# Block 1's small matmuls: heads and index scores in alternating row groups and banks, compression sums in column groups, attention in pairs of units

## The chip, the cores and the metric

The kernel runs on one core of one Trainium2 chip. The metric is the device time of one execution in microseconds; a time is the median of several runs. The profile is of one further execution, whose own time stands beside its span.

## The reference

Two transformer blocks on 256 tokens of width 1024, in float32. The change lies in the first block's mixer. Cut to what it touches:

```python
# DSA: index scores choose the 64 keys that each query of 8 heads attends to
s_h = einsum('bqhd,bsd->bqhs', qi, k_i)              # 8 index heads of width 32
score = einsum('bqh,bqhs->bqs', wi, relu(s_h))       # causal
_, idx = top_k(score, 64)
logits = einsum('bqhd,bqkd->bqhk', qa, k_a[idx]) / 8 + bias   # heads of width 64, one shared key
o_a = softmax(logits) @ v_a[idx]
# NSA: 8 heads of width 64 in two groups, each with its own keys; three branches, gated
k_cmp = gelu(blocks(kc) @ w1_k) @ w2_k               # 15 blocks of 32 tokens, stride 16; same for v
o_c = softmax(q @ k_cmp / 8 + bias) @ v_cmp
o_s = softmax(q @ k_s / 8 + bias) @ v_s              # all 4 blocks are selected at 256 tokens
o_w = softmax(q @ k_w / 8 + bias) @ v_w
mix = sigmoid(gate_a) * (o_a @ w_branch_a) + sigmoid(gate_b) * ((g0*o_c + g1*o_s + g2*o_w) @ w_branch_b)
```

## The kernel before, in words

Weights stream from HBM in units of two k-tiles (`stream_dma`, on SP's queue) into four raw buffers; ScalarE and VectorE split each into a rounded part `hi` (L262) and a remainder `lo` (L263). `gemm_feat` (L337) runs a chunk of 512 columns as 8 k-tiles, each of 4 feature tiles by 3 matmuls (`hi`·`xh`, `hi`·`xl`, `lo`·`xh`; L349, L351, L352) of 256 columns.

Small work is put between the gemms' k-tiles by hand: `later` appends jobs to a list, and a gemm takes one job off it behind each of its first seven k-tiles (`flush(1)`); `flush()` takes all that is left. In block 1 the input gemm's chunks run in the order 4, 0, 1, 3, 2 and then the four gate chunks 5 to 8. Jobs in their order:

- beside chunk 1 and on: eight `index(t, hp)` jobs, each with two matmuls of 32 rows (head group `hp` lies at partitions 32·hp), a relu on ScalarE and two score additions on VectorE; then eight `topk(r)` jobs on VectorE;
- appended behind chunk 1: `bias_job`, a matmul whose result `tv` goes to DRAM and comes back as the bias table `BT` by eight transfers of POOL's queue, followed on POOL by a memset and two copies into `cmpB`, which wait for those transfers;
- beside chunk 2: `cmp1(i, half)`, 16 accumulating matmuls of 30 columns for each of k and v, the gelu, whose output `ge` POOL clears first (L756), then `cmp2`;
- beside the gate chunks: `cq` (compressed logits), then the attention as `step(i)` over 18 units. A unit is two heads of 256 keys or four heads of 128 keys. `step(i)` runs `qk` of unit i (L835, 64 rows), `pv` of unit i-3 (L868) and `tr` of unit i-2 (transposes, L855). VectorE adds the bias and takes the maximum (L841), ScalarE takes the exponent (L846), VectorE copies the transposes (L857).

The order of instructions on TensorE, VectorE and ScalarE is planned from a simulated timeline, so it can deviate from the order of the code; POOL and SP keep the order of the code. PSUM's eight banks are three for gemm sums (`acc`), two for transposes (`tr`), two for small results (`sm`) and one for outputs (`o`). While `wide` is set, every other transpose group takes an `sm` bank (`ptr`).

Of the kernel before, what the change touches and what calls it, by code (L numbers as in the profile page):

```python
# [9 lines left out]
F32 = mybir.dt.float32  # L10
# [199 lines left out]
class Prog:  # L210
# [342 lines left out]
    def block1_mix(self, x0, x):  # L553
        tc, nc, ap, g = self.tc, self.nc, self.ap, self.g
        with ExitStack() as es, ExitStack() as rs_:
# [100 lines left out]
            def index(t, hp):  # L656
                n = 128 * (t + 1)
                pr = slice(32 * hp, 32 * hp + 32)
                ps = self.psm().rearrange("p (a b) -> p a b", a=2)
                for a in range(2):  # L660
                    nc.tensor.matmul(ps[:, a, :n], qi[pr, a, t * 128:t * 128 + 128], ki[pr, :n], start=True,
                                     stop=True)
                R = ip.tile([128, 2, 256], F32, tag="R", name="R")
                nc.scalar.activation(R[:, :, :n], ps[:, :, :n], AF.Relu, scale=1.0 / 16)
                if hp == 2:
                    cur[t] = caus[:, 256 - n:]
                for a in range(2):
                    h = hp + 4 * a
                    nx = ip.tile([128, 256], F32, tag="sc%d" % t, name="sc")
                    nc.vector.scalar_tensor_tensor(nx[:, :n], R[:, a, :n], wi(t, h), cur[t], op0=ALU.mult,  # L670
                                                   op1=ALU.add)
                    cur[t] = nx[:, :n]
# [19 lines left out]
            mp = rpool("cmpp", 1)  # L692
            cw = []
# [8 lines left out]
            def d1(i, ps):  # L702
# [3 lines left out]
                for i, nm in enumerate("kv"):  # L706
# [5 lines left out]
                    blk = mp.tile([128, 16, 2, 15], F32, name="blk" + nm)  # L712
                    for gr in range(2):
                        v = bass.AP(tensor=kp.tensor, offset=kp.offset + 256 * gr,
                                    ap=[list(kp.ap[0]), [2, 16], [16, 15]])
                        nc.gpsimd.tensor_tensor(blk[:, :, gr, :], v,
                                                cw[i][1][:, 0:16].unsqueeze(2).to_broadcast([128, 16, 15]),
                                                op=ALU.add)
# [60 lines left out]
            self.later(lambda: cmp1(0, 0), lambda: cmp1(0, 1), lambda: cmp1(1, 0), lambda: cmp1(1, 1),  # L779
# [25 lines left out]
            units = []  # L805
            for br in (1, 2, 0):
                for t in (1, 0):
                    nh = 2 if t else 4
                    for u in range(8 // nh):
                        if br == 0:  # L810
                            pr, fts = 64 * (u % 2), [nh * (u // 2) + i for i in range(nh)]
                            heads = [2 * f + u % 2 for f in fts]
                        else:
                            heads = [nh * u + i for i in range(nh)]
                            pr, fts = 64 * (heads[0] // 4), [h % 4 for h in heads]
                        units.append(dict(br=br, t=t, nh=nh, pr=pr, fts=fts, heads=heads, first=(u == 0),
                                          last=(u == 8 // nh - 1)))
# [10 lines left out]
            def qk(U):  # L828
                br, t, nh, pr = U["br"], U["t"], U["nh"], U["pr"]
                n, j0 = 128 * (t + 1), 128 - 128 * t  # L830
                q = qa if br == 0 else qb
                kk = ka[pr:pr + 64, :n] if br == 0 else kv[pr:pr + 64, 1 + br, :n]
                ps = self.psm().rearrange("p (a b) -> p a b", a=nh)
                for i in range(nh):
                    nc.tensor.matmul(ps[:, i, :], q[pr:pr + 64, U["fts"][i], t * 128:t * 128 + 128], kk, start=True,  # L835
                                     stop=True)
# [91 lines left out]
            extra = {2: [ct], 4: [lambda: cv(1), lambda: cv(0)]}  # L928
# [3 lines left out]
            nu = len(units)  # L932
            n_nsa = sum(1 for U in units if U["br"])
            for i in range(4):
                extra.setdefault(n_nsa + 4 + i, []).append(jb[i])
# [12 lines left out]
            for i in range(nu + 3):  # L948
                steps.append(lambda i=i: step(i))
# [14 lines left out]
            self.flush()  # L964
            for t in range(2):
# [616 lines left out]
```

## Time and profile before

| | us |
|---|---|
| median of 3 runs (1139.65 to 1142.34) | 1141.07 |
| profiled execution, its own time | 1140.78 |
| span of that execution | 1139.0 |
| TensorE busy in the span | 1112.4 (98%) |
| VectorE busy | 766.9 (67%) |
| ScalarE busy | 573.3 (50%) |
| POOL busy | 143.8 (13%) |

PE is TensorE's matmul row and PEld its weight loads, DVE is VectorE, ACT ScalarE. A busy PE is a pipeline with work in it, so the distance from one matmul's start to the next says more than a matmul's own duration. PEclk is the granted share of the full clock of 2.4 GHz.

### The profile page before, as it was taken

What the parts mean: (1) busy time and instruction counts of PE and PEld (TensorE: products, weight loads), DVE (VectorE), ACT (ScalarE), POOL (GpSimd) and SP (SyncE); (2) the same over time, 40 slices, a digit from 0 to 9 for tenths busy, and PEclk for the clock granted to TensorE, in tenths of its full rate; (3) what the DMA queues carried; (4) which work ended last, traced back from release to release, by engine and by line L of the source; (5) the groups of instructions that cost most, each with busy time, mean ns of one, the idle gap of its engine ahead of it and who ended that gap; (6) DMA issues with size and microseconds to landing.
All of it is one profiled execution on the core that took longest, in us unless ns stands there. A gap on an engine that the chain in (4) does not pass through costs nothing.

```text
span 1139.0 us, 17655 instructions
## 1 busy us (share of the span) xinstructions
PE 1112.4 (98%) x6848; PEld 993.6 (87%) x6848; DVE 766.9 (67%) x1208; ACT 573.3 (50%) x858; POOL 143.8 (13%) x145
## 2 busy tenths in 40 slices
PE   8989999999999999999999999999999999999997
PEld 8888899888888888888878998889999987888886
DVE  6755776778764568777457676556779777776644
ACT  6324454555544446555446335555555455655542
POOL 1411230000000010000001784000323000000000
PEclk9998999999999999999999999999999998999999
DMA  8792214655555655555555655434545455555552
GB/s 294 255 195 97 65 51 146 200 187 187 191 196 173 201 181 187 186 184 192 195 167 184 192 179 167 162 119 145 185 149 166 166 188 167 185 186 186 188 179 92
DMA packets 55876, 196.91 MB, mean 173 GB/s; under 512 B 6700, under 2 KB 6972, under 8 KB 55536
## 3 DMA queue, kind: packets, MB, share of 16 engines
q1 hardware_dynamic: 52704, 186.44, 49.9%
q0 software_dynamic: 2800, 9.21, 3.3%
q8 instruction: 54, 0.88, 0.3%
q14 instruction: 30, 0.25, 0.1%
q10 hardware_dynamic: 288, 0.14, 0.1%
HBM read 192.84 MB, written 1.44 MB: 171 GB/s over the span
## 4 chain that ended last, share of the span: by engine, by line
PE 85%; POOL 5%; DMA 4%; DVE 4%; ACT 1%; issue 1%; DVEq 0%; SPq 0%; POOLq 0%; ACTq 0%
PE acc L368 20%; PE acc L369 10%; PE acc L307 9%; PE acc L306 9%; PE acc L305 9%; PE acc L349 6%; PE acc L351 6%; PE acc L352 6%; PE sm L835 2%; POOL sw L1261 2%; DMA sw<-qkT 2%; POOL qkT L1262 2%; POOL qkT L1260 1%; PE o L868 1%; DVE lo L263 1%; DMA BT<-tvd 1%
## 5 line engine op out<-in xcount | busy, mean ns | idle before, releaser
L263 DVE TENSOR_TENSOR lo<-raw,hi 128x1024 fp32r<-128x1024 f32 (+2 forms) x356 | 450.0, 1267 | 272.1 <-ACT hi L262 270.2
L262 ACT ACTIVATE hi<-raw 128x1024 fp32r<-128x1024 f32 (+2 forms) x356 | 371.5, 1045 | 432.9 <-issue 133.4
L368 PE MATMUL acc<-xs,hi 128*128 128x512 f32 x960 | 340.3, 400 | 1.3 <-DVE sum L374 1.1
L369 PE MATMUL acc<-xs,lo 128*128 128x256 f32 x960 | 269.0, 281 | 1.6 <-DVE lo L263 1.6
L368 PEld LDWEIGHTS acc<-xs,hi 128*128 128x128 f32 x960 | 180.8, 189 | 44.6 <-DVE sum L374 1.3
L349 PE MATMUL acc<-xs,hi 128*128 128x256 f32 (+1 forms) x696 | 199.8, 289 | 0.3 <-ACT hi L262 0.3
L351 PE MATMUL acc<-xs,hi 128*128 128x256 f32 (+1 forms) x696 | 199.0, 287 | 0.0
L352 PE MATMUL acc<-xs,lo 128*128 128x256 f32 (+1 forms) x696 | 198.1, 287 | 0.1
L369 PEld LDWEIGHTS acc<-xs,lo 128*128 128x128 f32 x960 | 181.9, 189 | 2.3 <-DVE lo L263 1.9
L349 PEld LDWEIGHTS acc<-xs,hi 128*128 128x128 f32 (+1 forms) x696 | 133.6, 192 | 3.7 <-issue 2.5
L351 PEld LDWEIGHTS acc<-xs,hi 128*128 128x128 f32 (+1 forms) x696 | 133.7, 192 | 2.4 <-issue 2.0
L352 PEld LDWEIGHTS acc<-xs,lo 128*128 128x128 f32 (+1 forms) x696 | 132.9, 192 | 1.6 <-issue 1.0
L306 PE MATMUL acc<-lo,hT 128*128 128x512 f32 x304 | 118.5, 390 | 0.0
L307 PE MATMUL acc<-hi,hT 128*128 128x512 f32 x304 | 118.0, 389 | 0.0
L305 PE MATMUL acc<-hi,hT 128*128 128x512 f32 x304 | 117.8, 390 | 0.0
L307 PEld LDWEIGHTS acc<-hi,hT 128*128 128x128 f32 x304 | 57.1, 188 | 11.9
L305 PEld LDWEIGHTS acc<-hi,hT 128*128 128x128 f32 x304 | 57.1, 188 | 11.8
L306 PEld LDWEIGHTS acc<-lo,hT 128*128 128x128 f32 x304 | 57.1, 188 | 11.7
L305 PE MATMUL acc<-hi,xs 128*128 128x386 f32 (+1 forms) x128 | 48.6, 381 | 1.6 <-DVE f L1129 1.5
L306 PE MATMUL acc<-lo,xs 128*128 128x386 f32 (+1 forms) x128 | 47.9, 374 | 0.0
L307 PE MATMUL acc<-hi,xs 128*128 128x386 f32 (+1 forms) x128 | 47.0, 373 | 0.0
L374 DVE TENSOR_TENSOR sum<-acc,sum 128x512 f32<-128x512 f32 x60 | 41.1, 684 | 0.0
(421 smaller groups left out, 1396.6 us busy)
## 6 DMA issues: line engine op xcount, KB each, us to landing
raw<-in_w_in SPq DMA_DIRECT2D x100, 512.0 KB, 3.5
raw<-in_ffn_w_gate SPq DMA_DIRECT2D x44, 512.0 KB, 3.4
raw<-in_ffn_w_up SPq DMA_DIRECT2D x44, 512.0 KB, 3.3
raw<-in_ffn_w_down SPq DMA_DIRECT2D x44, 512.0 KB, 3.4
raw<-in_w_mlp_in SPq DMA_DIRECT2D x32, 512.0 KB, 3.4
raw<-in_w_mlp_out SPq DMA_DIRECT2D x32, 512.0 KB, 3.3
raw<-in_w_out SPq DMA_DIRECT2D x16, 512.0 KB, 3.5
raw<-in_w_in SPq DMA_DIRECT2D x16, 386.0 KB, 3.3
```

The costliest lines, as they stand in the source:

```text
L262: nc.scalar.activation(hi[:, :n * w], raw[:, :n * w], AF.Copy)
L263: nc.vector.tensor_tensor(lo[:, :n * w], raw[:, :n * w], hi[:, :n * w], op=ALU.subtract)
L305: nc.tensor.matmul(ps[t][:, :w], xh[:, k, sl], hi, start=(k == 0), stop=False)
L306: nc.tensor.matmul(ps[t][:, :w], xh[:, k, sl], lo, start=False, stop=False)
L307: nc.tensor.matmul(ps[t][:, :w], xl[:, k, sl], hi, start=False, stop=last)
L349: nc.tensor.matmul(o, hi[:, fs], xh[:, k, :], start=(k == 0 and f % 2 == 0), stop=False, skip_group_check=True)
L351: nc.tensor.matmul(o, hi[:, fs], xl[:, k, :], start=False, stop=False, skip_group_check=True)
L352: nc.tensor.matmul(o, lo[:, fs], xh[:, k, :], start=False, stop=last, skip_group_check=True)
L368: nc.tensor.matmul(ps[:, f, :, :], hi[:, fs], x.both[:, k, :, :], start=(k == 0), stop=False)
L369: nc.tensor.matmul(ps[:, f, 0, :], lo[:, fs], x.hi[:, k, :], start=False, stop=last)
L374: nc.vector.tensor_tensor(s, ps[:, :, 0, :], s, op=ALU.add)
L835: nc.tensor.matmul(ps[:, i, :], q[pr:pr + 64, U["fts"][i], t * 128:t * 128 + 128], kk, start=True, stop=True)
```

## The change

Four things are edited. `index` takes two head groups at once, each with a bank of its own, and issues their matmuls in turn, so that neighbours lie in different row groups. `cmp1` swaps stationary and moving operands: the 32 columns of a block (30 and two zeros) are loaded, the 128 columns of `w1` move, and the 16 partial products go to four column groups, l mod 4; `cmp1b` then adds the four groups up by a matmul with `fold`, four stacked identities that POOL copies at the start. The attention pairs units into nine duos whose two halves lie in the two row groups; `qk` issues their matmuls in turn into two banks, `step(i)` runs `pv` of duo i-2, `qk` of duo i and `tr` of duo i-1, each step is followed by one empty place or one transposition job, and `narrow()` keeps transposes off the `sm` banks until the gate chunks are done.

```diff
-            def index(t, hp):
+            def index(t, hps):
                 n = 128 * (t + 1)
-                pr = slice(32 * hp, 32 * hp + 32)
-                ps = self.psm().rearrange("p (a b) -> p a b", a=2)
+                pss = [self.psm().rearrange("p (a b) -> p a b", a=2) for _ in hps]
                 for a in range(2):
-                    nc.tensor.matmul(ps[:, a, :n], qi[pr, a, t * 128:t * 128 + 128], ki[pr, :n], start=True,
-                                     stop=True)
+                    for hp, ps in zip(hps, pss):
+                        pr = slice(32 * hp, 32 * hp + 32)
+                        nc.tensor.matmul(ps[:, a, :n], qi[pr, a, t * 128:t * 128 + 128], ki[pr, :n], start=True,
+                                         stop=True)
...
-                for hp in (2, 0, 1, 3):
-                    self.later(lambda t=t, hp=hp: index(t, hp))
+                for hps in ((2, 0), (1, 3)):
+                    self.later(lambda t=t, hps=hps: index(t, hps))
...
+            fold = mp.tile([128, 32], F32, name="fold")
+            for q in range(4):
+                nc.gpsimd.tensor_copy(fold[32 * q:32 * q + 32, :], self.ident[32 * q:32 * q + 32, 32 * q:32 * q + 32])
...
-                    blk = mp.tile([128, 16, 2, 15], F32, name="blk" + nm)
+                    blk = mp.tile([128, 16, 32], F32, name="blk" + nm)
+                    nc.gpsimd.memset(blk[:, :, 30:32], 0.0)
...
-            def cmp1(i, half):
+            def cmp1(i):
                 nm = "kv"[i]
-                if half == 0:
-                    cps[i] = self.psm()
-                ps = cps[i]
-                for l in range(8 * half, 8 * half + 8):
-                    nc.tensor.matmul(ps[:, :30], cw[i][0][:, l, :], blks[i][:, l, :, :].rearrange("p a b -> p (a b)"),
-                                     start=(l == 0), stop=(l == 15))
-                if half == 0:
-                    return
+                ps = self.psm()
+                for l4 in range(4):
+                    for q in range(4):
+                        l = 4 * l4 + q
+                        nc.tensor.matmul(ps[32 * q:32 * q + 32, :128], blks[i][:, l, :], cw[i][0][:, l, :],
+                                         start=(l4 == 0), stop=(l4 == 3), skip_group_check=True)
+                hq = mp.tile([128, 128], F32, name="hq" + nm)
+                nc.vector.tensor_copy(hq, ps[:, :128])
+                cps[i] = hq
+
+            def cmp1b(i):
+                nm = "kv"[i]
+                ps = self.psm()
+                nc.tensor.matmul(ps[:, :32], cps[i], fold, start=True, stop=True)
...
-            self.later(lambda: cmp1(0, 0), lambda: cmp1(0, 1), lambda: cmp1(1, 0), lambda: cmp1(1, 1),
+            self.later(lambda: cmp1(0), lambda: cmp1(1), None, lambda: cmp1b(0), lambda: cmp1b(1), None,
                        lambda: cmp2(0), lambda: cmp2(1))
...
+            duos = []
             for br in (1, 2, 0):
                 for t in (1, 0):
                     nh = 2 if t else 4
+                    for u in range(4 // nh):
+                        fts = [nh * u + i for i in range(nh)]
+                        duo = []
+                        for half in range(2):
+                            heads = [2 * f + half for f in fts] if br == 0 else [f + 4 * half for f in fts]
+                            duo.append(dict(br=br, t=t, nh=nh, pr=64 * half, fts=fts, heads=heads,
+                                            first=(u == 0 and half == 0), last=(u == 4 // nh - 1 and half == 1)))
+                        duos.append(duo)
...
+            def qk(duo):
+                pss = [self.psm().rearrange("p (a b) -> p a b", a=duo[0]["nh"]) for _ in duo]
+                for i in range(duo[0]["nh"]):
+                    for U, ps in zip(duo, pss):
+                        br, t, pr = U["br"], U["t"], U["pr"]
+                        n = 128 * (t + 1)
+                        q = qa if br == 0 else qb
+                        kk = ka[pr:pr + 64, :n] if br == 0 else kv[pr:pr + 64, 1 + br, :n]
+                        nc.tensor.matmul(ps[:, i, :], q[pr:pr + 64, U["fts"][i], t * 128:t * 128 + 128], kk,
+                                         start=True, stop=True)
+                for U, ps in zip(duo, pss):
+                    softmax(U, ps)
...
-            extra = {2: [ct], 4: [lambda: cv(1), lambda: cv(0)]}
+            extra = {1: [ct], 2: [lambda: cv(1), lambda: cv(0)]}
...
             def step(i):
-                if i + 2 < nu and units[i + 2]["br"] == 0:
-                    bm(units[i + 2])
-                if i < nu:
-                    qk(units[i])
-                if 0 <= i - 3 < nu:
-                    pv(units[i - 3])
-                if 0 <= i - 2 < nu:
-                    tr(units[i - 2])
+                if 0 <= i - 2 < nu:
+                    for U in duos[i - 2]:
+                        pv(U)
+                if i + 1 < nu and duos[i + 1][0]["br"] == 0:
+                    for U in duos[i + 1]:
+                        bm(U)
+                if i < nu:
+                    qk(duos[i])
+                if 0 <= i - 1 < nu:
+                    for U in duos[i - 1]:
+                        tr(U)
                 for e in extra.get(i, ()):
                     e()
-            for i in range(nu + 3):
-                steps.append(lambda i=i: step(i))
+            for i in range(nu + 2):
+                steps += [lambda i=i: step(i), jb[i - n_nsa - 2] if 0 <= i - n_nsa - 2 < 4 else None]
+            steps += jb[len(duos) - n_nsa:]
+            self.narrow()
             self.later(*steps)
...
             self.flush()
+            self.wide = True
```

## Rows read from the trace of the kernel before

**Rows 1.** The page: busy time of TensorE; its granted clock in 40 slices.

```profile
PE 1112.4 (98%) x6848; PEld 993.6 (87%) x6848; DVE 766.9 (67%) x1208; ACT 573.3 (50%) x858; POOL 143.8 (13%) x145
...
PEclk9998999999999999999999999999999998999999
```

**Rows 2.** Stretches: length, busy of PE, PEld, DVE, ACT, POOL, clock, DMA share, GB/s.

```profile
28.00:57.00 29.00, 29.00 (x208) 25.88 (x206) 22.97 (x49) 11.30 (x16) 13.15 (x24) 1.00 0.75 253
57.00:81.40 24.40, 24.40 (x204) 23.55 (x202) 16.14 (x49) 6.36 (x8) 5.40 (x10) 1.00 0.90 189
81.40:87.60 6.20, 0.12 (x2) 0.00 (x0) 0.22 (x3) 0.07 (x1) 0.91 (x5) 0.86 0.71 167
87.60:92.60 5.00, 4.97 (x39) 4.74 (x40) 2.18 (x3) 3.14 (x11) 0.27 (x1) 0.50 0.34 107
...
96.60:176.00 79.40, 79.40 (x585) 71.44 (x585) 56.65 (x175) 37.78 (x118) 18.70 (x16) 1.00 0.21 68
```

**Rows 3.** Waits of TensorE, 20 to 200 us: in all, times, longest.

```profile
PE sm L766 <- DVE gek L757: 6.1, 1, 6.1
```

**Rows 4.** Chain of waits, 58 to 90 us: start, length, what.

```profile
60.38 0.46 DVE tv L591
...
71.16 15.15 DMA BT<-tvd
...
86.69 0.38 POOL cmpB L600
...
87.29 0.07 POOL gek L756
...
87.63 0.40 PE sm L766 x4
88.03 0.56 PE sm L773 x16
```

**Rows 5.** Timeline of PE, 32 to 34 us: start, length, line, operation, count.

```profile
32.09 0.28 PE L351 MATMUL acc<-xs,hi 128*128 128x256 f32 x1
32.21 0.28 PE L352 MATMUL acc<-xs,lo 128*128 128x256 f32 x1
32.42 1.13 PE L661 MATMUL sm<-ki,qi 32*128 32x256 f32 x4
...
33.70 0.28 PE L351 MATMUL acc<-xs,hi 128*128 128x256 f32 x1
```

**Rows 6.** Timeline of PE around an index job of 128 columns.

```profile
42.45 0.28 PE L351 MATMUL acc<-xs,hi 128*128 128x256 f32 x1
42.66 0.71 PE L661 MATMUL sm<-ki,qi 32*128 32x128 f32 x4
...
43.52 0.28 PE L349 MATMUL acc<-xs,hi 128*128 128x256 f32 x1
```

**Rows 7.** Timeline of PE around the heads of one unit.

```profile
121.84 0.28 PE L352 MATMUL acc<-xs,lo 128*128 128x256 f32 x1
122.05 1.13 PE L835 MATMUL sm<-kv,qb 64*128 64x256 f32 x4
...
123.33 0.28 PE L351 MATMUL acc<-xs,hi 128*128 128x256 f32 x1
```

**Rows 8.** All head passes (L835): count, ns min/median/max, first and last start, forms.

```profile
L835 PE MATMUL sm<-kv,qb x64: 272/374/480, 96.6 to 142.3; 64*128 64x256 f32 x32, 64*128 64x128 f32 x32
...
L835 PE MATMUL sm<-ka,qa x32: 272/374/480, 144.9 to 165.1; 64*128 64x256 f32 x16, 64*128 64x128 f32 x16
```

**Rows 9.** The passes of cmp2's second half (L773), same columns.

```profile
L773 PE MATMUL sm<-csv,gev x16: 290/314/314, 88.0 to 88.3; 128*16 128x64 f32 x16
```

**Rows 10.** Timeline of PE around one half of a compression sum.

```profile
66.55 0.28 PE L352 MATMUL acc<-xs,lo 128*128 128x256 f32 x1
66.67 1.86 PE L743 MATMUL sm<-blkk,w1k 128*128 128x30 f32 x16
...
68.57 0.28 PE L351 MATMUL acc<-xs,hi 128*128 128x256 f32 x1
```

More of the change, by code (lines that the diff above doesn't have):

```diff
@@ L654, in block1_mix @@
             cur = {}
-            def index(t, hp):
+            def index(t, hps):
                 n = 128 * (t + 1)
-                pr = slice(32 * hp, 32 * hp + 32)
-                ps = self.psm().rearrange("p (a b) -> p a b", a=2)
+                pss = [self.psm().rearrange("p (a b) -> p a b", a=2) for _ in hps]
                 for a in range(2):
-                    nc.tensor.matmul(ps[:, a, :n], qi[pr, a, t * 128:t * 128 + 128], ki[pr, :n], start=True,
-                                     stop=True)
[L663 to L672, printed above, removed]
+                    for hp, ps in zip(hps, pss):
+                        pr = slice(32 * hp, 32 * hp + 32)
+                        nc.tensor.matmul(ps[:, a, :n], qi[pr, a, t * 128:t * 128 + 128], ki[pr, :n], start=True,
+                                         stop=True)
+                for hp, ps in zip(hps, pss):
+                    R = ip.tile([128, 2, 256], F32, tag="R", name="R")
+                    nc.scalar.activation(R[:, :, :n], ps[:, :, :n], AF.Relu, scale=1.0 / 16)
+                    if hp == 2:
+                        cur[t] = caus[:, 256 - n:]
+                    for a in range(2):
+                        h = hp + 4 * a
+                        nx = ip.tile([128, 256], F32, tag="sc%d" % t, name="sc")
+                        nc.vector.scalar_tensor_tensor(nx[:, :n], R[:, a, :n], wi(t, h), cur[t], op0=ALU.mult,
+                                                       op1=ALU.add)
+                        cur[t] = nx[:, :n]
             def topk(r):
@@ L808, in block1_mix @@
                     nh = 2 if t else 4
[L809 to L817, printed above, removed]
+                    for u in range(4 // nh):
[6 more added lines that the diff above has]
+                        duos.append(duo)
             box = {}
@@ L826, in bm, with softmax @@
                                         M[:, t, :n].unsqueeze(1).to_broadcast([128, nh, n]), op=ALU.add)
-            def qk(U):
-                br, t, nh, pr = U["br"], U["t"], U["nh"], U["pr"]
-                n, j0 = 128 * (t + 1), 128 - 128 * t
[L831 to L836, printed above, removed]
+            def qk(duo):
[10 more added lines that the diff above has]
+                    softmax(U, ps)
+            def softmax(U, ps):
+                br, t, nh = U["br"], U["t"], U["nh"]
+                n, j0 = 128 * (t + 1), 128 - 128 * t
                 L = U["L"] = lp.tile([128, nh, n], F32, tag="L", name="L")
@@ L931, in block1_mix @@
             ja = self.split_T(osrc(oa), range(4), [0, 1], *oaT)
[L932 to L935, printed above, removed]
+            nu = len(duos)
+            n_nsa = sum(1 for duo in duos if duo[0]["br"])
             def step(i):
-                if i + 2 < nu and units[i + 2]["br"] == 0:
-                    bm(units[i + 2])
-                if i < nu:
-                    qk(units[i])
-                if 0 <= i - 3 < nu:
-                    pv(units[i - 3])
-                if 0 <= i - 2 < nu:
-                    tr(units[i - 2])
+                if 0 <= i - 2 < nu:
[4 more added lines that the diff above has]
+                        bm(U)
+                if i < nu:
+                    qk(duos[i])
+                if 0 <= i - 1 < nu:
+                    for U in duos[i - 1]:
+                        tr(U)
                 for e in extra.get(i, ()):
                     e()
-            for i in range(nu + 3):
-                steps.append(lambda i=i: step(i))
+            for i in range(nu + 2):
+                steps += [lambda i=i: step(i), jb[i - n_nsa - 2] if 0 <= i - n_nsa - 2 < 4 else None]
+            steps += jb[len(duos) - n_nsa:]
+            self.narrow()
             self.later(*steps)
```

3 lines of the change are left out of this document (1 added, 2 removed).

## The prediction

> **What bounds the kernel now.** I read the page first: TensorE is busy 98% of the span, at full clock but for a few short dips [rows 1]. So a microsecond of TensorE work that goes away is a microsecond of the end, as long as nothing that TensorE then waits for takes its place. Everything that the change touches lies between 28 and 176 us, so the table by stretches comes next [rows 2]: from 28 to 81.4 and from 96.6 to 176 TensorE has no idle time; between 81.4 and 87.6 it does nothing, and in the 5 us behind that its granted clock is 0.50 (the 1.2 of its two levels, 1.2 and 2.4 GHz). The list of waits has one entry for TensorE in this part, 6.1 us for DVE's gek [rows 3]. The chain of waits tells what that is [rows 4]: the bias sums' result tv (60.4), its trip to DRAM, the transfers to BT, which land at 86.3, the POOL copy cmpB that waits for them, and behind it in POOL's queue the memset of gek (87.29). So the stage has two limits: TensorE's own work, and one chain from the bias matmul to cmp2. DVE is at 79% from 28 to 57 and at 71% in the attention (96.6 to 176) [rows 2].
>
> **What a short group of matmuls costs.** An fp32 matmul stands as two passes in the trace. In [rows 5] the gemm's matmuls start 0.12 us apart; with a group of four index passes between them two such starts lie 1.49 us apart (32.21 to 33.70), so the group costs 1.49 - 0.24 = 1.25. With half the columns it is 43.52 - 42.45 - 0.24 = 0.83 [rows 6]. The difference, 0.42 for 4 x 128 columns, gives 0.105 us for a pass of 128 columns and 0.21 for one of 256; what is left, 0.41, is paid once per group, for going into a row group and back. The heads of 64 rows cost the same, 123.33 - 121.84 - 0.24 = 1.25 for four passes [rows 7]; eight passes of 128 columns give 8 x 0.107 + 0.41 = 1.27. The records hold 48 passes of 256 and 48 of 128 columns [rows 8], that is 12 groups of four and 6 of eight.
>
> **Do two groups run side by side?** No row of before has two row groups in turn. The nearest is cmp2's second half: 16 passes of 64 columns that go over four column groups [rows 9]. At full clock 64 columns are half of 0.107; at the half clock of that stretch [rows 2] they are 0.107 again, so one after another would take 1.7 us. The chain has 0.56 for all 16 (88.03 in [rows 4]), and all start within 0.3 us: four run at once. I take that for the column groups of cmp1 and, as the nearest row, for the two row groups; the bounds are full overlap and none.
>
> **The parts, one by one.**
> *Heads (qk).* Before 12 x 1.25 + 6 x 1.27 = 22.6 us. After, nine duos have twice the passes each, in two row groups and two banks. With overlap a duo takes as long as one unit: 9 x 1.26 = 11.3, saved 11.3. Without it 6 x (8 x 0.21 + 0.41) + 3 x (16 x 0.107 + 0.41) = 18.9, saved 3.7.
> *Index scores.* Before 4 x 1.25 + 4 x 0.83 = 8.3. With overlap half, saved 4.1; without 2 x 2.09 + 2 x 1.25 = 6.7, saved 1.6. The first pair needs a ki copy that POOL's queue sends, where the first job before needed none; gemm matmuls cover that on TensorE, but DVE's score chain starts later by a part of the copy's trip, which has no row here. DVE has 6 us of slack in this stretch [rows 2]; I charge 1 us (0 to 3, half of the slack).
> *Compression sums.* Before, 16 passes cost 68.57 - 66.55 - 0.24 = 1.78 [rows 10], so 64 cost 7.1. After there are 2 x 32 passes of 128 columns, four abreast: 2 x (8 x 0.107 + 0.41) = 2.5, and two fold matmuls of two 32-column passes each, at 1.78 / 16 = 0.11 a pass and a hop out of the gemm, some 0.6 in all. Saved 4.0; without overlap 2 x (32 x 0.107 + 0.41) + 0.6 = 8.3, lost 1.2. DVE's two copies hq, POOL's four fold copies and two memsets are small and lie beside gemm matmuls; if the cover were gone they would cost under 1 us each.
> *Half as many steps.* Transposes and pv passes stay in number; they stand in groups twice as long, so half of the returns to the gemm fall away: 1 us (0 to 2).
> *Attention order.* A duo takes both sm banks at once, transposes lose their share of the sm banks (narrow), and tr follows its qk by one step instead of two. TensorE's stretch shrinks from 79.4 to about 67, while DVE's 56.65 us stay: 84% busy, with DVE in order (scores, PT copies, weight splits). Behind qk of a duo wait the next tr and pv. I charge 2.5 us of waits; bounds 0 and the whole gain, 11.3.
> *The BT chain.* This is the term that isn't in the diff. Jobs leave the pending list one per k-tile, seven per gemm. Before: 8 index and 8 topk jobs, so the bias job is the third of gemm 2. After: 4 index jobs fewer, so it is the sixth of gemm 3, five k-tiles (5 x 12 x 0.12 = 7.2 us) earlier in program order. The order that is planned need not follow that whole way, so I count 4 to 7 us, and up to 4 more as the index work shrinks: tv at about 52.5 instead of 60.4. From there to cmp2 it was 87.6 - 60.4 = 27.2 us. After, it also holds POOL's memsets of kcT and VB, which the bias job now stands ahead of (0.6 us, as they queue behind the BT wait), and it shares the DMA engines with a denser weight stream: they are at 90% from 57 to 81.4 already [rows 2]; I add 1 us (0 to 4). So cmp2 can start at about 81, some 7 us earlier. But TensorE also gets there earlier: from tv to cmp2's place it had 21.0 us of work (60.4 to 81.4), and that loses 4.0 with cmp1 unless more gate matmuls are put in front of cmp2. So the wait grows from 6.1 to about 9: +3, bounds -8.6 (wait and the half-clock stretch behind it, 2.5, both gone) and +8.
>
> **Sum.** The profiled execution took 1140.8 us (span 1139.0), 0.3 from the median 1141.1, so it stands for it. 1140.8 - 11.3 - 4.1 - 4.0 - 1.0 + 1.0 + 2.5 + 3.0 = 1126.9: I say 1127. Behind 176 TensorE has no wait on this part, so the gain should reach the end whole.
>
> **Rivals.**
> *Half overlap.* If passes start strictly in program order, the second pass of a matmul holds up the first pass of the next group: 8 passes take the time of 5, 16 that of 9. Then a duo takes 1.46 or 1.37 (+1.6 in all), index +0.6, cmp1 17 x 0.107 + 0.41 twice (+1.9): 1131. The 16 starts within 0.3 us of [rows 9] speak against it, since two at a time would need 9 x 0.107 = 0.96. The Trainium skill (TensorE: Matmul & The Clock Gate, Part 3) states such an order, matmuls starting and ending in strict program order; by that rule the time would be the one just worked out, and the trace agrees less with it than with full overlap.
> *Row groups don't overlap at all*, only column groups do: heads +7.6, index +2.5, and TensorE is then slow enough that the 2.5 of waits go: 1134.5. For it: no row shows two row groups at once.
> *DVE and ACT pace the attention.* If every duo step waits 1 us on the way from scores over DVE, ACT and the PT copy to pv, that is 9 us instead of 2.5: 1133.5. For it: one step of lag instead of two, DVE at 84%. Against: before it has 23 us free in this stretch and TensorE never waits.
> *The BT wait goes*, because the chain starts 8 us earlier and the plan fills the gap: 1127 - 3.0 - 8.6 = 1115. Against: both ends of the wait move together.
> *Slower: each change of row group pays a switch.* If an alternation costs c, each duo of four matmuls pays 4c, each of eight 8c, and nothing overlaps. Against before, with 0.2 of a group's 0.41 left at its ends, the heads change by 48c - 5.3, the index by 16c - 2.4; cmp1's gain is offset by the BT wait and DVE (-4 + 3 + 1). It decides from c = 0.12; with c = 0.2, half of a group's fixed cost, the time is 1146. Against: in [rows 9] a change of column group shows no such price. The Trainium skill (TensorEngine Tiling (Array Packing), Tiling Modes) states that a change of tiling mode drains TensorE and a change of tile doesn't; no run here shows that for row groups.
>
> **Chances and range.** Forecast 0.50; half overlap 0.13; no row overlap 0.12; DVE-paced 0.12; the wait gone 0.07; slower 0.06. The range from 1115 to 1137 takes in all but the slower case and most of the unknown bounds (waits and BT together can add 10 to the forecast). Faster by over 0.2% (2.3 us, about what a measurement here can tell): 0.90; within it 0.04; slower 0.06.
>
> **What would show it.** Starts of the head passes in pairs, a duo of four in about 0.85 us from first to last start; no more than 10 us of TensorE waits between 92 and 170; cmp1 in about 0.9 us per sum; tv at about 52.5, BT landed at about 80 and a TensorE wait of about 9 us that ends there, with a half-clock stretch behind it; DVE at 80 to 85% in the attention. It is wrong if the head passes start 0.1 or 0.2 us apart one by one, if TensorE waits for DVE or ACT in every step, or if the wait for gek is gone or twice as long.

## The result, and the profile after

| | median us | ratio to before, with interval |
|---|---|---|
| before | 1141.7 | |
| after | 1134.8 | 0.9925 [0.9905, 0.9945] |
| after, run again (a_again) | 1135.5 | 0.9942 [0.9923, 0.9962] |

By the two ratios the change gains 8.6 and 6.6 us; forecast were 14. The first execution of after, the profiled one, took 1562.8 us at a lowered clock and is left out of the ratio (without it the median is 1133.8); all that follows is read from the profile of a_again: the same kernel, span 1133.3 us where before had 1139.0. Each ratio is taken against executions of before from the same series, whose medians were 1141.5 to 1142.8 us, so kernels of two series are better compared by their ratios than by their medians.

> The changed kernel once more, for a profile at full clock. Theory 1 (pairs pulled apart): the two halves of most pairs stand one behind the other on TensorE, so all index groups and the first seven duos start their passes 0.21 us (256 columns) or 0.11 us (128) apart, one by one, at the old price of about 1.25 us a half; only the last two duos start in pairs, some 0.03 us apart. Heads then cost about 20 us instead of 22.6 and the index 8.3 as before. Theory 2 (row groups don't overlap on the chip): passes stand one by one in the last two duos as well. Theory 3 (the wait for the bias table eats the gain): TensorE's wait for gek is 9 to 12 us instead of 6.1. Time 1131 to 1136 by all three.

**The stretches** (page, then the table by stretches, columns as in [rows 2]):

```profile
PE 1108.0 (98%) x6852; PEld 987.6 (87%) x6852; DVE 767.7 (68%) x1210; ACT 573.2 (51%) x858; POOL 145.2 (13%) x151
...
28.00:57.00 29.00, 29.00 (x201) 25.11 (x201) 23.06 (x49) 11.13 (x15) 12.99 (x28) 1.00 0.77 254
57.00:81.50 24.50, 24.47 (x249) 23.61 (x247) 16.99 (x52) 6.71 (x8) 4.87 (x9) 1.00 1.00 195
81.50:85.30 3.80, 0.00 (x0) 0.00 (x0) 0.24 (x3) 2.11 (x2) 1.45 (x7) 0.75 0.96 333
85.30:90.30 5.00, 4.99 (x39) 4.76 (x40) 3.08 (x5) 2.36 (x11) 0.25 (x1) 0.51 0.51 167
94.00:168.00 74.00, 74.00 (x560) 66.65 (x560) 52.69 (x172) 35.66 (x114) 18.13 (x14) 1.00 0.22 72
```

TensorE is as busy as before. In the attention (94 to 168) it never waits, and DVE is at 52.69 of 74.0, 71% as before: the attention got shorter by 5, not by 12. Only 2.2 of these 5 us are the heads (table below); gemm work also moved out of the stretch, since 439 of the matmuls of `gemm_feat` start ahead of cmp2, where in before 402 did. The idle stretch ahead of cmp2 is still there, 3.8 us instead of 6.2, and so is the half clock behind it, 5 us at 0.51, which costs 2.5 us as before.

**The wait and its chain** (list of waits of TensorE, 20 to 200 us, then the chain of waits), against [rows 3] and [rows 4]:

```profile
PE sm L782 <- DVE gek L773: 3.8, 1, 3.8
...
55.46 5.50 DMA tvd<-tv
...
61.25 3.98 POOL BT L596 x7
65.23 18.25 DMA BT<-tvd
83.85 0.38 POOL cmpB L600
...
84.51 0.46 POOL VB L742
85.06 0.20 DVE gek L773
85.31 0.40 PE sm L782 x4
```

In the chain of before tvd's transfer stands at

```profile
61.12 5.84 DMA tvd<-tv
```

The chain starts 5.7 us earlier, as forecast, but cmp2 starts only 2.3 us earlier (85.31, before 87.63): BT's transfer now takes 18.25 us from its last issue to its landing, where it took 15.15. The stretch from 57 us on has a DMA share of 1.00 instead of 0.90. During the transfer itself the share was near 1 in both (1.02 and 0.98); what differs is that the queue of the weights moved 1.90 MB beside it, where in before it moved 1.05. The memset of VB (84.51) is in the chain too. TensorE comes to cmp2 at 81.5 us in both kernels, and its wait got shorter, so theory 3 is out.

**The small matmuls** (timeline of TensorE: an index job, one half of a pair, the other half, a pair in turns, a compression sum), against [rows 5], [rows 7] and [rows 10]:

```profile
32.01 0.28 PE L352 MATMUL acc<-xs,lo 128*128 128x256 f32 x1
32.22 1.13 PE L663 MATMUL sm<-ki,qi 32*128 32x256 f32 x4
33.27 0.38 PE L349 MATMUL acc<-xs,hi 128*128 128x256 f32 x1
...
116.43 1.13 PE L853 MATMUL sm<-kv,qb 64*128 64x256 f32 x4
117.49 0.98 PE L879 MATMUL tr<-ident,L 128*128 128x128 f32 x7
118.40 1.13 PE L853 MATMUL sm<-kv,qb 64*128 64x256 f32 x4
...
140.95 0.28 PE L352 MATMUL acc<-xs,lo 128*128 128x256 f32 x1
141.16 1.13 PE L853 MATMUL sm<-ka,qa 64*128 64x256 f32 x8
142.22 0.39 PE L349 MATMUL acc<-xs,hi 128*128 128x256 f32 x1
...
63.25 0.28 PE L352 MATMUL acc<-xs,lo 128*128 128x256 f32 x1
63.45 1.08 PE L752 MATMUL sm<-w1v,blkv 128*32 128x128 f32 x32
64.47 0.39 PE L349 MATMUL acc<-xs,hi 128*128 128x256 f32 x1
```

This is the main reading. The first index job stands where it stood, with 4 passes. The pair that starts at 116.43 comes as 4 passes, transposes, and 4 more passes. Only the pair at 141.16 is what the diff writes: 8 passes in the time of 4 (1.13 us). The order in which TensorE gets its instructions is planned by readiness and not by the text of the program. All eight index groups and most of the nine pairs of head units were pulled apart: of the 48 couples that the 96 head passes can form (one pass of either half), 12 start together (0.007 us apart).

### The profile page after: what moved, and what is told of

The parts are those of the page before. It is cut to its first block, busy times and chain, and to the rows that moved or that the text cites. A ratio compares the mean times of both kernels' runs of the same rounds, so it can differ in the third digit from the quotient of the medians.

```text
span 1560.7 us, 17674 instructions
## 1 busy us (share of the span) xinstructions
PE 1544.9 (99%) x6852; PEld 1241.7 (80%) x6852; DVE 773.5 (50%) x1210; ACT 575.0 (37%) x858; POOL 138.0 (9%) x151
## 4 chain that ended last, share of the span: by engine, by line
PE 98%; DVE 1%; ACT 0%; DMA 0%; issue 0%; DVEq 0%; SPq 0%; ACTq 0%
PE acc L368 20%; PE acc L305 10%; PE acc L306 10%; PE acc L369 10%; PE acc L307 10%; PE acc L349 9%; PE acc L351 9%; PE acc L352 9%; PE sm L853 2%; PE o L892 2%; PE tr L879 1%; PE sm L1381 1%; PE o L1411 1%; PE tr L399 1%; PE sm L663 1%; PE sm L1519 1%
## 5 line engine op out<-in xcount | busy, mean ns | idle before, releaser
L368 PE MATMUL acc<-xs,hi 128*128 128x512 f32 x960 | 465.1, 507 | 0.8 <-DVE x L1027 0.6
L369 PE MATMUL acc<-xs,lo 128*128 128x256 f32 x960 | 331.5, 346 | 0.8 <-DVE lo L263 0.8
L349 PE MATMUL acc<-xs,hi 128*128 128x256 f32 (+1 forms) x696 | 243.6, 351 | 0.0
L351 PE MATMUL acc<-xs,hi 128*128 128x256 f32 (+1 forms) x696 | 243.2, 350 | 0.0
L352 PE MATMUL acc<-xs,lo 128*128 128x256 f32 (+1 forms) x696 | 240.7, 350 | 0.0
L369 PEld LDWEIGHTS acc<-xs,lo 128*128 128x128 f32 x960 | 208.1, 217 | 2.3 <-DVE lo L263 1.3
L349 PEld LDWEIGHTS acc<-xs,hi 128*128 128x128 f32 (+1 forms) x696 | 175.1, 252 | 4.9 <-issue 4.3
L351 PEld LDWEIGHTS acc<-xs,hi 128*128 128x128 f32 (+1 forms) x696 | 175.5, 252 | 3.7 <-issue 3.3
L352 PEld LDWEIGHTS acc<-xs,lo 128*128 128x128 f32 (+1 forms) x696 | 175.9, 254 | 2.5 <-issue 2.1
L306 PE MATMUL acc<-lo,hT 128*128 128x512 f32 x304 | 154.5, 508 | 0.0
L307 PE MATMUL acc<-hi,hT 128*128 128x512 f32 x304 | 153.9, 507 | 0.0
L305 PE MATMUL acc<-hi,hT 128*128 128x512 f32 x304 | 153.3, 507 | 0.0
L307 PEld LDWEIGHTS acc<-hi,hT 128*128 128x128 f32 x304 | 63.0, 207 | 35.8 <-issue 11.5
L305 PE MATMUL acc<-hi,xs 128*128 128x386 f32 (+1 forms) x128 | 61.8, 484 | 1.4 <-DVE f L1157 1.4
L307 PE MATMUL acc<-hi,xs 128*128 128x386 f32 (+1 forms) x128 | 59.9, 475 | 0.0
```

The lines of the kernel that those rows point to most:

```text
L305: nc.tensor.matmul(ps[t][:, :w], xh[:, k, sl], hi, start=(k == 0), stop=False)
L306: nc.tensor.matmul(ps[t][:, :w], xh[:, k, sl], lo, start=False, stop=False)
L307: nc.tensor.matmul(ps[t][:, :w], xl[:, k, sl], hi, start=False, stop=last)
L349: nc.tensor.matmul(o, hi[:, fs], xh[:, k, :], start=(k == 0 and f % 2 == 0), stop=False, skip_group_check=True)
L351: nc.tensor.matmul(o, hi[:, fs], xl[:, k, :], start=False, stop=False, skip_group_check=True)
L352: nc.tensor.matmul(o, lo[:, fs], xh[:, k, :], start=False, stop=last, skip_group_check=True)
```

## What the kernel's instructions cost, in one table

For each run: the price of the index and head groups and of the compression sums (with the fold), summed from the records (from the last start ahead of a group to the first start behind it, less 0.107 us; about 0.08 per group below the prediction's way, which goes on to the second start); the couples of head passes that start together, of 48; TensorE's wait in block 1; when cmpB's first copy starts, some 0.4 us behind BT's landing; and how much earlier than before block 1 ends (start of the 900th matmul of the gemms, 196.2 in before). A dash: the groups hold a wait or lie at half clock, so the sum tells nothing.

| run | ratio [interval] | index | heads | couples | sums | wait | cmpB | block 1 |
|---|---|---|---|---|---|---|---|---|
| before | 1 | 7.6 | 21.4 | 0 | 6.8 | 6.1 | 86.7 | 0 |
| a_again | 0.9942 | 7.6 | 19.2 | 12 | 2.5 | 3.8 | 83.9 | -9.2 |
| b_turns | 0.9939 [0.9920, 0.9959] | 5.0 | 16.6 | 32 | 2.5 | 10.5 | 88.1 | -8.0 |
| c_cmp | 1.0007 [0.9990, 1.0025] | 7.6 | 20.8 | 2 | 3.0 | 9.9 | 90.4 | -0.8 |
| d_attn | 0.9975 [0.9959, 0.9990] | 7.6 | 16.9 | 24 | 6.8 | 6.3 | 87.6 | -3.5 |
| f_hoist | 0.9884 [0.9863, 0.9906] | 7.6 | - | 24 | 2.5 | 4.0 | 84.9 | -12.8 |
| g_turns_hoist | 0.9902 [0.9873, 0.9930] | 5.0 | - | 28 | 2.5 | 5.0 | 83.4 | -14.0 |
| h_early | 0.9887 [0.9862, 0.9912] | 7.6 | 18.0 | 22 | 2.6 | 2.1 | 81.0 | -13.8 |
| i_early_turns | 0.9886 [0.9859, 0.9913] | 5.0 | - | 32 | 2.9 | 3.8 | 84.1 | -11.3 |
| l_gate | 0.9902 [0.9881, 0.9923] | 4.5 | 15.1 | 34 | 2.5 | 8.4 | 86.8 | -12.0 |
| j_gate | 0.9902 [0.9883, 0.9921] | 4.5 | - | 32 | 2.5 | 7.0 | 85.0 | -13.5 |
| k_gate_early | 0.9877 [0.9854, 0.9899] | 4.5 | 15.7 | 32 | 2.6 | 3.4 | 80.6 | -16.6 |
| m_before_early | 0.9914 [0.9897, 0.9931] | 7.6 | 21.3 | 0 | 6.8 | 0 | 79.2 | -8.7 |

## Experiments: one part of the change at a time

**Only the compression sums** (the hunks of fold, blk, cmp1 and cmp1b put into before).

> The kernel before with the compression sums alone changed (four column groups, fold matmul, empty places). Index and attention are as before. Theory 3: 4 us less work on TensorE in front of the wait for gek, and the wait grows from 6.1 to about 10; the time is that of before, 1140 to 1142. If the wait stays at 6, the 4 us arrive: 1137. In both the 32 passes of a sum take 0.9 to 1.4 us instead of 3.6; were column groups not to overlap, 3.4 to 3.8.

Measured 1142.3 us, no change (1.0007), as theory 3 had it. The sums did get cheaper, 6.8 to 3.0 us. The chain of waits and the list of waits of TensorE:

```profile
60.30 0.46 DVE tv L591
...
71.06 19.01 DMA BT<-tvd
90.44 0.38 POOL cmpB L600
...
91.37 0.40 PE sm L779 x4
...
PE sm L779 <- DVE gek L770: 9.9, 1, 9.9
```

tv is where it was (60.30), BT's transfer takes 19.01 us instead of 15.15, and the wait is 9.9 instead of 6.1: 3.8 saved, 3.8 waited. But TensorE does not come to cmp2 earlier. Start of cmp2 less the wait is 81.5 in both (91.37 - 9.9 and 87.63 - 6.1), because 434 matmuls of `gemm_feat` now start ahead of cmp2, where 402 did. What is later is the end of the wait, by 3.7 us, and that is BT. Had BT landed as in before, by this count the 3.8 us would have been gained. BT's transfer had more company, 1.60 MB of weights beside it instead of 1.05; that this slowed it fits, but no run tests it by itself.

**Only the attention** (the hunks from units to step put into before).

> The kernel before with the attention alone changed (duos, one step of lag, no transposes on the small banks). Everything up to the wait for gek is as before, so the wait is 6 us. Theory 1: the heads' gain comes from the few duos whose halves stand in turn (here three to five of nine), 3 to 6 us: 1135 to 1138. Theory 2: 2 to 4 us from fewer groups only, 1137 to 1139. If DVE paced it, TensorE would show waits for DVE between 96 and 176 and the gain would be under 2 us.

Measured 1139.1 us, a gain of 0.25%, just above the ranges of both theories. Here half of the couples stand together (24 of 48), the heads cost 4.5 us less, and the wait at cmp2 is the old one (6.3). The attention lies behind the wait, so what it saves stays.

**The change, with its pairs chained in turns** (each matmul is held behind the one before it, and the second half goes first):

```
+                mm = None
                 for i in range(duo[0]["nh"]):
-                    for U, ps in zip(duo, pss):
+                    for U, ps in list(zip(duo, pss))[::-1]:
...
+                        with tc.issue_after(mm.ins) if mm else ExitStack():
+                            mm = nc.tensor.matmul(ps[:, i, :], ...)
```

and likewise in index.

> The changed kernel with each matmul of a pair of index groups or of a duo's heads held behind the one before it, so that the halves stand in turn on TensorE. Theory 1: passes of the two halves start in pairs, a duo costs about 1.3 to 1.7 us instead of 2.5, the index pairs 1.3 to 1.7 instead of 2.5; 5 to 9 us faster than the changed kernel, about 1126, less what the wait for gek grows by (the index lies before it). Theory 2: passes one by one, each change of row group costs a switch, 0 to 8 us slower than the changed kernel. Theory 3: heads faster as in theory 1, but the wait for gek longer by what the index saves (about 3 us).

Measured 1133.8 us: not to be told from a_again (the intervals overlap nearly whole). The order did change: 32 couples, heads 2.6 and index 2.6 us cheaper. But the wait for gek grew from 3.8 to 10.5, so 5.2 were saved and 6.7 more were waited, over twice what theory 3 had. TensorE comes to cmp2 2.5 us earlier, and BT lands 4.2 us later (87.7, a_again 83.5). A second thing shows in the timeline of TensorE:

```profile
103.67 0.70 PE L857 MATMUL sm<-kv,qb 64*128 64x256 f32 x2
104.29 0.39 PE L351 MATMUL acc<-xs,hi 128*128 128x256 f32 x1
...
104.96 1.13 PE L857 MATMUL sm<-kv,qb 64*128 64x256 f32 x6
```

The first matmul of a pair starts alone and the other three (6 passes) follow four gemm matmuls later, so the pair enters and leaves the row groups twice: by the table's way 0.73 and 1.16 us, where a whole pair costs 1.17. Eight of the nine pairs are broken like this. It is not a wait for a bank: DVE's last read of either bank had ended at 102.15, ahead of both pieces, and the same holds for every broken pair of this run. The break lies in the planned order.

## Experiments: the wait behind the bias table

Three readings stood against each other. A: the wait for gek, which stands behind BT's copies in POOL's queue, holds what the pairs save. B: the stretch from 66 to 85 us, with a DMA share of 1.0, is paced by the transfers, and a wait taken away comes back. C: only the order of the halves matters.

**The memsets ahead of the bias table** (f_hoist): kcT, VB and both ge are set before bias_job is queued, so that cmp2 no longer stands behind cmpB's copies.

```
+            ges = [mp.tile([128, 2, 16], F32, name="ge" + nm) for nm in "kv"]
+            for ge in ges:
+                nc.gpsimd.memset(ge, 0.0)
             self.later(bias_job)
...
-                ge = mp.tile([128, 2, 16], F32, name="ge" + nm)
-                nc.gpsimd.memset(ge, 0.0)
+                ge = ges[i]
```

(kcT and VB with their memsets move to the same place.)

> The changed kernel, with the memsets of kcT, VB, gek and gev put ahead of the bias table's transfers in GpSimd's queue, so that gek no longer stands behind the copies of cmpB, which wait for BT's transfer. Everything else is as written in the changed kernel; since the planner counts anew, 6 or 7 of the 9 pairs of head units now come out in turns, where 2 did. Theory A (the wait of TensorE at cmp2 for gek, 3.8 us and 6.8 us at half clock behind it, holds what the pairs save): the wait at cmp2 disappears, TensorE waits at most for cmpB's readers, and the time falls from 1135.5 to 1127 to 1131. Theory B (the stretch from 66 to 85 us, with a DMA share of 1.0, is paced by the transfers): the wait comes back as one for weights or for BT, time 1134 to 1136. Theory C (it is the order of the halves alone that costs): the pairs in turns give the 2 us that b_turns gave in block 1 and nothing from the wait, 1133 to 1134.

Measured 1129.4 us. The chain of waits:

```profile
64.81 19.69 DMA BT<-tvd
...
84.88 0.38 POOL cmpB L600
...
85.50 0.36 DVE Lc L919 x2
...
86.00 2.30 PE sm L855 x8
```

cmp2 and cq run before BT lands; now the first heads wait, 4.0 us, for a bank that Lc reads (DVE adds cmpB to the compressed logits there), and Lc needs cmpB. So the wait came back, as B says, though the work of cmp2 and cq has moved ahead of it; the time lies in the range of A. Another part of the gain is a side effect: with the new order the plan leaves 24 couples together instead of 12. The two can't be told apart in this run.

**The same with chained pairs** (f_hoist and b_turns together):

> f_hoist and b_turns together: the small matmuls of each pair chained so that they are issued in turns, and the four memsets ahead of the bias table's transfers. Theory A: the wait at cmp2, which had grown to 10.5 us in b_turns and took its savings, is gone or under 4 us; the time is 1123 to 1128. Theory B (transfers pace 66 to 85 us): the wait of 10 us comes back under another name, 1133 to 1135. Theory C: no more than b_turns, 1133 to 1134.

Measured 1130.5 us, between theories A and B and no better than f_hoist: the wait is 5.0 us, index saves 2.6 and heads are in turns in 28 couples where f_hoist had 24 already.

**The bias table earlier** (h_early): f_hoist, and rest and rb are loaded at the start, bias_job is queued ahead of the index jobs, and its transfers to BT are issued right behind chunk 1.

```
+            self.later(bias_job)
             for t in (1, 0):
                 for hps in ((2, 0), (1, 3)):
...
-            self.later(bias_job)
+            bias_load()
             self.gemm_feat(W_IN1, 3, *xT, dq(qb))
```

(bias_load holds the lines of bias_job from the loop over BT on.)

> f_hoist with the bias table begun earlier: its operands loaded at the start of the kernel, its matmul, its sum and the store of tvd put right behind the first projection, and BT's transfers called right after the second projection (some 13 us earlier than in the changed kernel). Theory A: BT's 18 us lie at about 52 to 68 us, nothing in block 1 waits for it, the clock does not fall there; 1125 to 1130. Theory B: the same bytes pass through the same queues earlier, so that what waits is now the weights of the third and fourth projection, 1133 to 1136. Theory C: 1133 to 1135.

Measured 1128.9 us, in the range of A, though not as A had it: BT lands at 80.6 us, not at 68. TensorE waits 2.1 us for gev, which stands behind a unit of weights whose transfer took 16.30 us, and its clock stays at 1.00 from 28 us to the end of block 1; both together account for 6.5 of the 8.6 us (6.1 of wait, 2.5 of half clock) that before lost there.

**The same with chained pairs:**

> h_early with the small matmuls of each pair chained in turns. Theory A: the sum of both, 1121 to 1127, that is what the prediction had counted for the change (its terms without the wait). Theory B: 1132 to 1135. Theory C: 1132 to 1134, as b_turns.

Measured 1129.4 us, between A and B: no gain over h_early. Its start was 2.3 us late in the profiled execution (150th gemm matmul), it waited 1.8 and 1.9 us in two places, and behind the second its clock fell to 0.5.

**The kernel before, with nothing but the early bias table and the hoisted memsets:**

> The kernel before, with nothing of the change but the bias table begun early and the four memsets hoisted, as in h_early: it asks what the wait of 6.1 us at cmp2 and the half clock behind it were worth by themselves. Theory A: both go, 6 to 9 us, 1133 to 1136.5. Theory B (the wait only moves to the next consumer of the same transfers): 1140 to 1143.

Measured 1131.5 us, 0.9914 [0.9897, 0.9931], below the range of theory A. This is the sharpest of the runs: without any of the change, moving one chain and four memsets gains 10 us, no less than the whole change (0.9925 and 0.9942, whose intervals overlap with this one). At the end of block 1 it is 8.7, what the wait and the half clock had cost (8.6). Turned round: with this chain moved, the whole change (h_early, 0.9887 [0.9862, 0.9912]) can't be told from none of it. TensorE has no wait at cmp2 at all. The table by stretches and POOL's timeline:

```profile
57.00:75.00 18.00, 18.00 (x157) 18.00 (x156) 13.22 (x46) 4.36 (x5) 0.82 (x2) 1.00 1.04 167
75.00:95.00 20.00, 20.00 (x163) 18.13 (x163) 12.67 (x41) 8.91 (x25) 1.08 (x3) 1.00 0.64 198
...
53.00 4.50 POOL L602 DMA_DIRECT2D BT<-tvd  x8
...
79.20 0.39 POOL L606 COPY cmpB<-BT 128x120 f32<-128x120 f32 x1 [21.38 <-DMA BT<-tvd]
```

The transfers were issued 14 us earlier than in before (53.00 against 67.25) and had landed 7.5 us earlier (cmpB at 79.2 against 86.7): beside a DMA share of 1.04 they took 21.88 us instead of 15.15. That was enough. The memsets have a part in it: cmp2 starts at 76.4, ahead of BT's landing, which it could not if gek still stood behind cmpB's copies.

## Experiments: whole pairs

**Both banks first** (l_gate): the change, with the matmuls of a pair chained and the first of them waiting for the readers of both banks.

```
+    def behind(self, mm):
+        for i in self.reads:
+            self.tc.add_manual_dep(mm.ins, i.name, mybir.DependencyInfo(mybir.DependencyClass.Sync,
+                                   mybir.DependencyReason.DATA), reason="both banks")
+        self.reads = []
...
+                        self.behind(mm)
```

(reads holds the last reading instruction of each half of the pair before.)

> The changed kernel with its pairs kept whole: the small matmuls of a pair are chained in their alternating order, and the first of them waits until both banks have been read empty, so that no half can begin alone. This is what the prediction had priced. By the matmul starts of the runs so far, a whole pair costs TensorE what one half cost alone (1.17 us for 256 columns, 1.19 for 128): index 7.6 to 3.8 us, heads some 7 us below the changed kernel. Theory A (what is saved ahead of cmp2 is given to the wait for gek, which stands behind the bias table; what is saved behind it stays): wait 7 to 10 us where the changed kernel has 3.8, time 1127 to 1130. Theory B (the turns are worth only what b_turns showed, the groups' ends taking the rest): 1132 to 1135.

Measured 1130.05 us: the upper edge of theory A. By the ratios, 0.9902 [0.9881, 0.9923], it is apart from a_again (0.9942, from 0.9923 on) but not from the first run of after (0.9925 [0.9905, 0.9945]). This is the kernel nearest to the one that the prediction priced. A pair that stays whole, the wait, and the stretches around it:

```profile
126.17 0.28 PE L351 MATMUL acc<-xs,hi 128*128 128x256 f32 x1
126.38 1.14 PE L865 MATMUL sm<-kv,qb 64*128 64x256 f32 x8
127.44 0.39 PE L352 MATMUL acc<-xs,lo 128*128 128x256 f32 x1
127.66 0.28 PE L349 MATMUL acc<-xs,hi 128*128 128x256 f32 x1
...
PE sm L792 <- DVE gek L783: 8.4, 1, 8.4
...
80.00:88.30 8.30, 0.01 (x2) 0.01 (x2) 1.48 (x4) 2.11 (x2) 1.47 (x7) 0.67 1.03 257
88.30:93.30 5.00, 5.00 (x40) 4.76 (x41) 2.94 (x5) 4.17 (x13) 0.85 (x2) 0.52 0.50 168
```

From 126.17 to 127.66 is 1.49, the same as around one half in [rows 5]: by the prediction's way 1.25 us for a pair, as priced. The wait is 8.4 us, about the 9 that were forecast: TensorE comes to cmp2 1.6 us earlier than in a_again, and BT lands 3.0 us later. Only two of the nine pairs of heads are whole like this one; seven are still broken once, by gemm matmuls, transposes or a pv group, and each break costs another way in and out. Of the index pairs three of four are whole.

**Both banks first, memsets hoisted:**

> l_gate with the memsets of kcT, VB, gek and gev ahead of the bias table's transfers, as in f_hoist (1129.4). Theory A: the index scores' 3.8 us go into the wait for cmpB's readers (4.0 us in f_hoist, then 6 to 8), the heads' 4 to 6 us stay: 1123 to 1126. Theory B: 1129 to 1131, as f_hoist and g_turns_hoist.

Measured 1130.8 us, theory B: the wait at Lc is 7.0 us where f_hoist has 4.0. Here BT lands at the same time in both (84.6 and 84.5), and TensorE comes to the wait 2.9 us earlier: what whole pairs save ahead of that place is waited there.

**Both banks first, bias table early:**

> l_gate with the bias table begun early, as in h_early (1128.9), where TensorE waited 2.1 us and its clock did not fall. Theory A: the pairs' savings are kept in full up to a wait of 3 to 5 us at cmp2 or cq: 1119 to 1124. Theory B (block 1 can't go below what its weights and the chain of the compression take): 1128 to 1131, the wait comes back, longer.

Measured 1126.1 us, the lowest median of all, 0.9877 [0.9854, 0.9899]; above the 1119 to 1124 of theory A and below theory B. It is faster than the changed kernel in both its runs (their intervals begin at 0.9905 and 0.9923), but not to be told from f_hoist, h_early and i_early_turns, and its interval just meets that of m_before_early (from 0.9897 on). The chain of waits shows what is late next:

```profile
59.38 16.00 DMA raw<-in_w_in
75.48 1.06 ACT hi L262
76.57 1.23 DVE lo L263
...
78.26 0.20 DVE gev L793
78.51 0.42 PE sm L809 x16
```

Not BT any more, but a unit of weights whose transfer takes 16.00 us beside BT's; its splits on ACT and DVE stand ahead of thv and gev, for which TensorE waits 3.4 us. So B holds in part: the same bytes go through the same queues, and something else comes late. This wait is shorter than the 8.4 us of l_gate.

## Why the prediction was right in sign and some 7 us too hopeful

That the time lies in the range is luck: 1134.8 is almost the 1134.5 of *Row groups don't overlap at all*, while the records show that they overlap. The terms, in us:

| term | priced | a_again | l_gate (both banks first) |
|---|---|---|---|
| heads | -11.3 | -2.2 | -6.3 |
| index | -4.1 | 0.0 | -3.1 |
| compression sums | -4.0 | -4.3 | -4.3 |
| waits in the attention | +2.5 | 0 | 0 |
| wait for gek | +3.0 | -2.3 | +2.3 |

(Differences of the table above; priced with 22.6 and 8.3 where the table's way gives 21.4 and 7.6.) In a_again they give -8.8, with a start 0.2 earlier -9.0; measured at the end of block 1 is -9.2. In l_gate -11.4, with 0.1 of start -11.5, measured -12.0. So half as many steps, priced at -1.0, has at most 0.5 left.

- **Heads and index: the step that failed.** The prices per pair were right (a whole pair costs what one half cost). Wrong was that the pairs would be executed as they are written. Only 12 of 48 couples were, and no index pair: of the 15.4 us priced for both, 2.2 came. That the change doesn't do what it says was not among my rivals. That the order is the reason, b_turns and l_gate show: with the matmuls chained, 32 and 34 couples start together, and index and heads get 5.2 and 7.2 us cheaper than in a_again. What in the plan pulls the pairs apart stays open. A candidate is the second half's bank, if the plan has it free later; but with both banks asked for (l_gate against b_turns, which also differ in which half goes first) the heads still stand in 16 pieces instead of 20, where whole pairs would be 9, and in b_turns no piece waited for a bank. The rest of l_gate's shortfall against 11.3 is pairs that still break.
- **Full overlap: right.** The first starts of two halves lie 0.007 us apart and 8 passes of 256 columns start within 0.76 us, as 4 do (0.75). *Half overlap* and *no row overlap* are out: by them a pair of four matmuls would take 1.46 or 2.1. The Trainium skill (TensorE: Matmul & The Clock Gate, Part 3) has matmuls start and end in strict program order; the slowdown that I had worked out from it isn't seen here, since the passes start in twos. Which half each record belongs to, and so whether the order itself holds, the records don't tell.
- **Switching row groups: no price.** The rival with 1146 is out for the same reason. The Trainium skill (TensorEngine Tiling (Array Packing), Tiling Modes) has TensorE drain at a change of tiling mode, not at one of tile alone; 0.007 us between the halves' starts agrees. (In that rival's sum 5.3 should read 5.6, which moves its time by 0.3.)
- **Compression sums: right in size** (priced 4.0, measured 4.3), but in c_cmp, by themselves, they brought nothing to the end of the kernel.
- **Attention waits: 0, not 2.5.** In a_again DVE stayed at 71%, as TensorE's stretch did not shrink to 67. But in l_gate it did (the heads take from 97.7 to 155.5 us, where before they took from 96.6 to 165.1), DVE is at 74% (48.62 of 66.00 us from 96 to 162), and there is no wait either: the term was too large, and *DVE and ACT pace the attention* is out.
- **BT chain: the chain was seen, the sizes weren't.** I had tv at 52.5, cmp2 at 81 and a wait of 9. tv came at 54.6 and cmp2 at 85.3, with a wait of 3.8: the chain from tvd's DMA to cmp2 took 29.9 us where it had 26.5, mostly BT's slower transfer (18.25). I had TensorE at cmp2 at 72; it came at 81.5, since the index had not shrunk and 37 more gemm matmuls (4.4 us at 0.12) were put ahead of cmp2, as much as the sums saved. In l_gate the wait is 8.4.
- **Behind 176 us: not whole.** Of the 9.2 us at the end of block 1, 5.7 reached the end. The MLP's matmuls, which the change doesn't touch, came 2% slower in one stretch, 143 of a kind in 50 us where before had 146, at a granted clock of 1.00 in both (groups of TensorE from 250 to 300 us, before and then a_again):

```profile
L368 PE MATMUL acc<-xs,hi 128*128 128x512 f32 x146 | 50.7, 394 | 0.0
...
L368 PE MATMUL acc<-xs,hi 128*128 128x512 f32 x143 | 50.6, 399 | 0.0
```

  that is 1.5 us between 230 and 320, and in the second mixer the wait for qkT was 3.6 us instead of 2.0, with another 0.5 just ahead. The first shows in a_again, c_cmp, i_early_turns, l_gate and j_gate, and not in the others. Its cause stays open, and so does what one execution of each can tell of it.

## What to carry to other kernels

Writing matmuls in turns is not enough where instructions are ordered by readiness: look in the trace whether the pairs start together, and chain them if they don't (12 couples became 32; asking for all banks first made it 34). Work saved ahead of a wait can come back as a longer wait in two ways: the engine comes to it earlier (j_gate), or what it waits for comes later (c_cmp); compare both ends of the wait. Follow its chain to the start and move that first. Here one small matmul, its way through DRAM to BT and four memsets, moved forward, brought as much as the whole rewrite. The lowest median was reached with both, though not clear of the early chain alone.

## What the runs showed of the hardware

- Fp32 passes in two row groups and two banks overlap in full: starts 0.007 us apart, 8 passes in the 1.13 us of 4. Over four column groups 32 passes of 128 columns took 1.08 us. Going from the gemm into such a group and back costs each time: a pair of 8 passes cost 1.17 us whole, and 0.73 and 1.16 us when broken into 2 and 6 (b_turns).
- The same eight transfers to BT, 256 KB each, took from 15.15 us (before) to 22.29 us (b_turns) from the last issue to landing, with a DMA share of 0.97 to 1.04 all that time. In the two runs where they took least (before 15.15, d_attn 15.37) the queue of the weights moved 1.05 and 1.04 MB beside them; in c_cmp (19.01) it moved 1.60, in the others (17.81 to 22.29) 1.88 to 2.24.
- TensorE's granted clock was at its lower level (0.50 to 0.52 of 2.4 GHz) for 5 us behind cmp2 after the idle 6.2 us of before, the 3.8 of a_again and the 8.3 of l_gate; in k_gate_early, after a wait of 3.4 us, it was 0.61 over 4 us. It stayed at 1.00 in m_before_early, which had no wait there, and in h_early, which had one of 2.1 us (TensorE from 80 to 85 us in h_early: length, busy, clock, DMA share, GB/s):

```profile
80.00:85.00 5.00, 5.00 (x43) 1.00 0.86 318
```
